# Gate and up projections of a feed-forward network: nine of eleven block pairs as seven products of quarters

## The chip, the cores and the metric

The kernel runs on one core of a Trainium2 chip. The metric is device time in microseconds (us) from one launch: 2508.59 us is the median of three runs of the kernel before (2506.43 to 2508.60). The profile is of one further execution.

## The reference

Two layers of a decoder trunk work on x of 512 tokens by 1024 features, all in float32. Each layer applies, with an RMS norm before and after each part, a feed-forward network (FFN), a hybrid token mixer (sparse attention and retention), cross-attention into 256 memory tokens, and a second FFN. What is changed here is the FFN:

```
def swiglu(x, w_gate, w_up, w_down):            # 1024 -> 2816 -> 1024
    return (jax.nn.silu(x @ w_gate) * (x @ w_up)) @ w_down
y = swiglu(rms_norm(x, pre_g), w_gate, w_up, w_down)
x = x + 0.5 * rms_norm(y, post_g)
```

There are four FFNs in all (two in each of two layers).

## The kernel before, in words

x lies in eight tiles of 128 features by 512 tokens (`x[c]`, features on the partitions), so a matmul has 128 x 128 weights as its stationary and up to 512 tokens as its moving operand. To keep float32 accuracy on a rounded type each operand is split into a high and a low part, and each product is three matmuls into one PSUM accumulation: high x high, high x low, low x high (`mm3`, L113 to L116).

Weights come as raw tiles of 128 x 1024 float32 (512 KB). `unit` (L79 to L87) loads one through SyncE's DMA queue into one of three `raw` buffers, ScalarE makes the high part `whi` (L85), and VectorE the low part `wlo` by a subtraction (L86); there are four buffers of each. GpSimd has no part in it.

`ffn` (L257 to L304) goes over the 22 blocks of 128 hidden features in three groups of 8, 7 and 7 (`GROUPS`). For a block it loads a gate unit and an up unit (8 slices of 128 x 128 each) and does 24 matmuls for each of the two, 48 of 512 columns. VectorE then multiplies both sums by the row norm `bc` (L274, L278), ScalarE takes a tanh (L276), VectorE finishes the SwiGLU (L279, L280), and the result is split into `hh` and `hl` (L122, L123). After a group the down projection adds the group's blocks to the eight tiles `y[c]`: units of 128 x 1024 or 128 x 896, one for each c, with 24 or 21 matmuls. In the last group each finished `y[c]` is squared on ScalarE and added up, mostly by GpSimd (`sumsq`, L145 to L155); `postnorm` (L205 to L213) makes the norm from it, updates x (VectorE `yn`, GpSimd `x`) and splits x for the next stage (`split_x`, L178 to L184). In the last FFN of the kernel `down_halves` does the last group for each half of the tokens apart, so that the first half's norm and output lie beside the second half's matmuls; its first block is also done in two halves of the tokens.

A stage before an FFN can leave it a `filler`: projections of memory keys or values that PE can do while the norm is made.

The order on each engine isn't the order of the text. A scheduler takes, at build time and with durations that it assumes, the instruction that comes first in the program among those that are ready and have a buffer; each engine then runs its list strictly in order. So work runs ahead as far as buffers reach: three `raw`, four `whi` and `wlo`, eight PSUM banks, and 24, 16 and 16 tiles of 128 x 512 in the classes "b", "xs" and "h".

Of the kernel before, what the change touches and what calls it, by code (L numbers as in the profile page):

```python
# [9 lines left out]
F32 = mybir.dt.float32  # L10
# [15 lines left out]
GROUPS = ((0, 8), (8, 15), (15, 22))  # L26
# [21 lines left out]
def trunk(ctx: ExitStack, tc: tile.TileContext, a: dict, out: bass.AP):  # L48
# [9 lines left out]
    slots = {"b": 24, "xs": 16, "h": 16, "kv": 6}  # L58
# [54 lines left out]
    def mm3(ps, ah, al, bh, bl, start, stop):  # L113
        pe.matmul(ps, ah, bh, start=start, stop=False)  # L114
        pe.matmul(ps, ah, bl, start=False, stop=False)  # L115
        pe.matmul(ps, al, bh, start=False, stop=stop)  # L116
# [40 lines left out]
    def rms_cols(ssq, n, width):  # L157
# [27 lines left out]

    def gcols(l, col):
        return small[l][:, col : col + NC]

    def prenorm():

        xh, xl = [h for h, _ in xs], [lo for _, lo in xs]
        xs.clear()
        ssq, part = None, None
# [9 lines left out]
        return xh, xl, cols, bc  # L203

    def postnorm(y, ssq, gains, nxt, ts_=slice(0, T)):  # L205

        w = ts_.stop - ts_.start
        ps = row_bc(rms_cols(ssq[:, ts_], D, w), w // P)
        for c in range(NC):
# [3 lines left out]
            split_x(c, nxt, ts_)  # L213
# [43 lines left out]
    def ffn(l, which, gains, nxt, filler=None, prep=None, halves=False):  # L257
        gu, dn = FF_UNITS[which]
        if filler:
            filler()  # L260
        xh, xl, cols, bc = prenorm()
        y, ssq = [None] * NC, None
        for gi, (f0, f1) in enumerate(GROUPS):
            hh, hl = [], []
            for f in range(f0, f1):
                w = [first.pop(b) if b in first else unit(a[gu][l, f, b], 1024) for b in range(2)]
                pss = [acc("ps_gu") for _ in range(2)]
# [18 lines left out]
            if prep and last:  # L286
                prep()
# [555 lines left out]
    for c in range(NC):  # L843
        split_x(c, gcols(0, G_F1PRE))
# [98 lines left out]
```

## Time and profile before

| | |
|---|---|
| median of three runs | 2508.59 us |
| the profiled execution | 2508.29 us, span 2506.5 us |
| PE busy | 2431.5 us (97%), 12052 matmuls |
| VectorE, ScalarE, GpSimd busy | 1400.2 (56%), 902.4 (36%), 258.8 us (10%) |
| DMA | 233.62 MB, mean 93 GB/s |
| TensorE clock granted | 0.995 in the mean |

All times in views are microseconds from the span's start. PE is TensorE's matmuls, PEld its weight loads, DVE is VectorE, ACT ScalarE, POOL GpSimd, SP SyncE. Matmuls overlap in the records, so their pace is read from the distance between starts. The FFNs take most of the span: their bodies lie at about 9 to 372, 900 to 1250, 1285 to 1635 and 2150 to 2490 us.

### The profile page before, as it was taken

The page shows a single profiled execution, that of the slowest core. Times are in us where ns is not written, and L with a number is a line of the kernel's source. Part 1 is how long each engine was busy: PE and PEld are TensorE (multiplying, and loading weights), DVE is VectorE, ACT ScalarE, POOL GpSimd, SP SyncE. Part 2 cuts the span into 40 slices and gives each one's busy share as a digit, 9 for nine tenths or more (in the row PEclk, how much of TensorE's full clock was granted, in tenths as well). Part 3 has the DMA queues.
Part 4 walks back from the last instruction along what each step waited for, and adds up shares of the span by engine and source line. Part 5 has one row for each costly group of instructions (what it writes and reads, how often), then busy time and mean ns, then how long its engine had stood idle before and what let it go on. Part 6 is the DMA issues. An engine that isn't in the chain of part 4 may idle for free. (4 is left out here: it accounts for less than half of the span.)

```text
span 2506.5 us, 30782 instructions
## 1 busy us (share of the span) xinstructions
PE 2431.5 (97%) x12052; PEld 2020.5 (81%) x12052; DVE 1400.2 (56%) x2536; ACT 902.4 (36%) x1480; POOL 258.8 (10%) x218
## 2 busy tenths in 40 slices
PE   8999999999999999999999999999999998999997
PEld 6888878888877878888878888868888777888887
DVE  6434458465776484344484344584657766634454
ACT  4322243255344443222343222332553443322222
POOL 0000022001040120000120000130010402100002
PEclk9999999999999999999999999999999999999999
DMA  4333333411232233233333333324112222232321
GB/s 173 98 100 94 99 121 108 143 45 34 76 109 84 93 101 93 101 93 100 110 98 96 101 93 101 106 89 150 44 35 70 93 76 68 86 100 92 102 90 62
DMA packets 74593, 233.62 MB, mean 93 GB/s; under 512 B 8272, under 2 KB 17744, under 8 KB 74448
## 3 DMA queue, kind: packets, MB, share of 16 engines
q1 hardware_dynamic: 65232, 222.21, 27.9%
q10 hardware_dynamic: 9216, 9.44, 1.2%
q8 instruction: 95, 1.56, 0.3%
q14 instruction: 50, 0.41, 0.1%
HBM read 229.53 MB, written 2.10 MB: 92 GB/s over the span
## 5 line engine op out<-in xcount | busy, mean ns | idle before, releaser
L85 ACT ACTIVATE whi<-raw 128x1024 fp32r<-128x1024 f32 (+2 forms) x402 | 417.8, 1041 | 1097.6 <-PE ps_gu L115 324.0
L86 DVE TENSOR_TENSOR wlo<-raw,whi 128x1024 fp32r<-128x1024 f32 (+2 forms) x402 | 491.2, 1223 | 292.7 <-ACT whi L85 284.4
L114 PE MATMUL ps_gu<-xsh,whi 128*128 128x512 f32 (+1 forms) x1424 | 552.3, 389 | 13.8 <-ACT whi L85 9.3
L115 PE MATMUL ps_gu<-xsl,whi 128*128 128x512 f32 (+1 forms) x1424 | 555.0, 390 | 9.9 <-DVE xsl L184 9.7
L116 PE MATMUL ps_gu<-xsh,wlo 128*128 128x512 f32 (+1 forms) x1424 | 552.8, 388 | 0.0
L115 PEld LDWEIGHTS ps_gu<-xsl,whi 128*128 128x128 f32 x1424 | 268.6, 189 | 71.2 <-DVE xsl L184 17.7
L114 PEld LDWEIGHTS ps_gu<-xsh,whi 128*128 128x128 f32 x1424 | 269.0, 189 | 69.2 <-ACT whi L85 9.2
L116 PEld LDWEIGHTS ps_gu<-xsh,wlo 128*128 128x128 f32 x1424 | 268.8, 189 | 55.4 <-DVE wlo L86 1.8
L154 POOL TENSOR_TENSOR ssq<-ssq,sq 128x512 f32<-128x512 f32 (+1 forms) x84 | 131.4, 1564 | 1708.7 <-ACT sq L153 1705.6
L115 PE MATMUL ps_dn<-hl,whi 128*128 128x512 f32 (+1 forms) x704 | 268.5, 382 | 2.4 <-DVE hl L123 2.4
L114 PE MATMUL ps_dn<-hh,whi 128*128 128x512 f32 (+1 forms) x704 | 268.2, 381 | 0.0
L116 PE MATMUL ps_dn<-hh,wlo 128*128 128x512 f32 (+1 forms) x704 | 268.0, 381 | 0.0
L278 DVE TENSOR_TENSOR u<-ps_gu,rstd_bc 128x512 f32<-128x512 f32 x88 | 60.8, 691 | 215.4 <-PE ps_gu L116 215.3
L274 DVE TENSOR_TENSOR g<-ps_gu,rstd_bc 128x512 f32<-128x512 f32 x88 | 60.8, 691 | 183.9 <-PE ps_gu L116 179.4
L115 PEld LDWEIGHTS ps_dn<-hl,whi 128*128 128x128 f32 x704 | 132.3, 188 | 28.9 <-DVE hl L123 3.8
L114 PEld LDWEIGHTS ps_dn<-hh,whi 128*128 128x128 f32 x704 | 132.4, 188 | 26.2 <-ACT hh L122 0.5
L116 PEld LDWEIGHTS ps_dn<-hh,wlo 128*128 128x128 f32 x704 | 132.4, 188 | 25.1
L301 DVE TENSOR_TENSOR y<-ps_dn,y 128x512 f32<-128x512 f32 x56 | 38.7, 691 | 132.3 <-PE ps_dn L116 132.3
L115 PE MATMUL ps_fm<-xsl,whi 128*128 128x512 f32 x256 | 103.2, 404 | 4.0 <-DVE xsl L184 3.8
L114 PE MATMUL ps_fm<-xsh,whi 128*128 128x512 f32 x256 | 103.0, 404 | 0.0
L116 PE MATMUL ps_fm<-xsh,wlo 128*128 128x512 f32 x256 | 101.3, 396 | 0.6 <-DVE wlo L86 0.6
L612 ACT ACTIVATE p<-p,smx 128x512 f32<-128x512 f32 (+3 forms) x128 | 70.5, 552 | 87.2 <-DVE smx L610 87.0
(226 smaller groups left out, 3723.0 us busy)
## 6 DMA issues: line engine op xcount, KB each, us to landing
raw<-in_ffn_gu_dram SPq DMA_DIRECT2D x176, 512.0 KB, 3.3
raw<-in_ffn_dn_dram SPq DMA_DIRECT2D x64, 448.0 KB, 3.3
raw<-in_ffn_dn_dram SPq DMA_DIRECT2D x32, 512.0 KB, 3.5
raw<-in_win_fm_dram SPq DMA_DIRECT2D x32, 512.0 KB, 3.3
raw<-in_wk_dram SPq DMA_DIRECT2D x16, 512.0 KB, 3.5
raw<-in_cmp_w_dram SPq DMA_DIRECT2D x16, 512.0 KB, 3.7
raw<-in_wout_dram SPq DMA_DIRECT2D x16, 512.0 KB, 3.5
raw<-in_wv_dram SPq DMA_DIRECT2D x16, 512.0 KB, 3.5
```

The source lines that it names most:

```text
L85: act.activation(hi, raw, AF.Copy)
L86: dve.tensor_tensor(lo, raw, hi.bitcast(F32), op=ALU.subtract)
L114: pe.matmul(ps, ah, bh, start=start, stop=False)
L115: pe.matmul(ps, ah, bl, start=False, stop=False)
L116: pe.matmul(ps, al, bh, start=False, stop=stop)
L154: eng.tensor_tensor(acc_t, acc_t, sq, op=ALU.add)
L274: dve.tensor_tensor(g1, pss[0], bc, op=ALU.mult)
L278: dve.tensor_tensor(u1, pss[1], bc, op=ALU.mult)
L301: dve.tensor_tensor(y[c], ps, y[c], op=ALU.add)
L612: act.activation(pr[i], pr[i], AF.Exp, bias=m, scale=-1.0, accum_out=sums[:, i : i + 1])
```

## The change

A pair of blocks is a 2 x 2 matrix of quarters: its rows are the two blocks, its columns the two halves of the 1024 inputs, and a quarter holds gate and up weights of 4 slices each, 128 x 1024 in all. x is a 2 x 2 matrix as well: halves of the inputs by halves of the tokens. Winograd's form of Strassen's scheme multiplies two such matrices with seven products of quarters instead of eight, and with sums of quarters before and after.

- `Pair` does this for nine of the eleven pairs of each FFN. Each product is 24 matmuls of 256 columns into one PSUM bank (gate in one half of it, up in the other). The sums of weights are made in place in the raw tiles by GpSimd: c + d into a new tile u, then c += a, u += a, u += b. Each of the seven raw tiles is then split as before. Partial results are kept by a copy on ScalarE (`kept`) or accumulate in PSUM, and VectorE and GpSimd combine them.
- The first two pairs of each FFN are plain: 48 matmuls of 256 columns for the first half of the inputs and 24 of 512 for the second, per block. While they run, `combos` makes the sums of x that the seven products need.
- The SwiGLU multiplies only the gate by the norm of the row; the factor that the up part lacks is put into the norm after the FFN (`cols` in `rms_cols`).
- The down projection comes in groups of four blocks and a last one of two. A group is done after the products of the following pair, and that pair's SwiGLU comes behind it. A unit of down weights now holds two c (or four).
- Buffers: six `raw` instead of three; "b" 18, "xs" 24, "h" 8. To fit, the mixer keeps q and ksel in raw tiles, and some of its and the attention's tiles move to "xs".
- The filler and the first two weight splits of the next FFN are now called at the start of the `postnorm` before it (`nxt[0]`).
- `down_halves` has two blocks instead of seven. The layout of the gate and up weights in DRAM follows the quarters.

```diff
-    slots = {"b": 24, "xs": 16, "h": 16, "kv": 6}
+    slots = {"b": 18, "xs": 24, "h": 8, "kv": 6, "onsa": 1}
...
-    def unit(src, n):
-        raw = wp.tile([P, 1024], F32, name="raw", tag="raw", bufs=3)[:, :n]
+    def raw_unit(src, n):
+        raw = wp.tile([P, 1024], F32, name="raw", tag="raw", bufs=6)[:, :n]
         nc.sync.dma_start(raw, src)
+        return raw
+    def split_unit(raw, n=1024):
         hi = wp.tile([P, 1024], F32R, name="whi", tag="whi", bufs=4)[:, :n]
         lo = wp.tile([P, 1024], F32R, name="wlo", tag="wlo", bufs=4)[:, :n]
         act.activation(hi, raw, AF.Copy)
         dve.tensor_tensor(lo, raw, hi.bitcast(F32), op=ALU.subtract)
         return hi, lo
-    def raw_unit(src, n):
-        raw = wp.tile([P, 1024], F32, name="raw", tag="raw", bufs=3)[:, :n]
-        nc.sync.dma_start(raw, src)
-        return raw
+    def unit(src, n):
+        return split_unit(raw_unit(src, n), n)
...
+    def split_s(c, g, ts_=slice(0, T)):
+        k = c % 4
+        for u, half in enumerate(HALVES):
+            if half.start < ts_.start or half.stop > ts_.stop:
+                continue
+            if c < 4:
+                if k % 2 == 0:
+                    ops["t", u] = big("x1h", F32R, tag="xs"), big("x1l", F32R, tag="xs")
+                ops[u + 1, k] = hi, lo = [t[:, HALVES[k % 2]] for t in ops["t", u]]
+                act.activation(hi, x[c][:, half], AF.Copy, scale=g[:, c : c + 1])
+                dve.scalar_tensor_tensor(lo, x[c][:, half], g[:, c : c + 1], hi.bitcast(F32), op0=ALU.mult, op1=ALU.subtract)
+        if c >= 4:
+            if ts_.start == 0:
+                ops["x", k] = big("x3h", F32R, tag="xs"), big("x3l", F32R, tag="xs")
+            hi, lo = [t[:, ts_] for t in ops["x", k]]
+            act.activation(hi, x[c][:, ts_], AF.Copy, scale=g[:, c : c + 1])
+            dve.scalar_tensor_tensor(lo, x[c][:, ts_], g[:, c : c + 1], hi.bitcast(F32), op0=ALU.mult, op1=ALU.subtract)
+            ops[3, k], ops[4, k] = [tuple(t[:, u] for t in ops["x", k]) for u in HALVES]
+    def combos(g):
+        sums = []
+        h7 = big("x7h", F32R, shape=(P, 4, T), tag="onsa")
...
+        for k in range(4):
+            b = []
+            for c in (k, k + 4):
+                xg = big("xg")
+                act.activation(xg, x[c], AF.Copy, scale=g[:, c : c + 1])
+                b += [xg[:, HALVES[0]], xg[:, HALVES[1]]]
+            t5, t7 = big("xt"), big("xt")
+            dve.tensor_tensor(t5[:, :256], b[1], b[0], op=ALU.subtract)
+            pool.tensor_tensor(t7[:, :256], b[3], b[1], op=ALU.subtract)
+            dve.tensor_tensor(t5[:, 256:], b[3], t5[:, :256], op=ALU.subtract)
+            pool.tensor_tensor(t7[:, 256:], t5[:, 256:], b[2], op=ALU.subtract)
+            put(5, k, t5, big("x5h", F32R, tag="xs"), big("x5l", F32R, tag="xs"))
+            sums.append(t7)
+        for k in range(4):
+            put(7, k, sums[k], h7[:, k], big("x7l", F32R, tag="xs"))
...
+    def postnorm(y, ssq, gains, nxt, ts_=slice(0, T), cols=None):
...
+        if ts_.start == 0 and nxt[0]:
+            nxt[0]()
...
+        def add(self, t, u):
+            pool.tensor_tensor(t, t, u, op=ALU.add)
+            return t
+        def raw(self, n):
+            if n == 1:
+                self.a = self.load(0)
+                return self.a
+            if n == 5:
+                self.c, self.d = self.load(2), self.load(3)
+                self.u = wp.tile([P, 1024], F32, name="raw", tag="raw", bufs=6)
+                pool.tensor_tensor(self.u, self.c, self.d, op=ALU.add)
+                return self.u
+            if n == 2:
+                self.b = self.load(1)
+                return self.b
+            if n == 7:
+                return self.add(self.c, self.a)
+            if n == 6:
+                return self.add(self.u, self.a)
+            if n == 3:
+                return self.add(self.u, self.b)
+            return self.d
+        def product(self, n, ps, o, start=True):
+            if n not in self.w:
+                self.weights(n)
+            wh, wl = self.w.pop(n)
+            for u in range(2):
+                for k in range(4):
+                    s = slice(u * 512 + k * P, u * 512 + (k + 1) * P)
+                    xh, xl = ops[o, k]
+                    mm3(ps[:, HALVES[u]], wh[:, s], wl[:, s], xh, xl, start and u == 0 and k == 0, u == 1 and k == 3, not start)
+        def kept(self, ps):
+            t = big("gk")
+            act.activation(t, ps, AF.Copy)
+            return t
...
+            for q in range(2):
+                k0 = "q", 2 * f + q
+                wh, wl = self.w.pop(k0) if k0 in self.w else split_unit(self.load(2 * f + q))
+                for k in range(4):
+                    for u in range(2):
+                        s = slice(u * 512 + k * P, u * 512 + (k + 1) * P)
+                        if q == 0:
+                            for i, half in enumerate(HALVES):
+                                mm3(pss[u][:, half], wh[:, s], wl[:, s], *ops[i + 1, k], i == k == 0, False)
+                        else:
+                            mm3(pss[u], wh[:, s], wl[:, s], *ops["x", k], False, k == 3)
...
+        def p1(self):
+            self.A = acc("ps_gu")
+            self.product(1, self.A, 1)
+            self.s1 = self.kept(self.A)
+        def p2(self):
+            self.product(2, self.A, 3, start=False)
+        def p7(self):
+            self.C = aux("ps_gc")
+            self.product(7, self.C, 7)
+            self.s7 = self.kept(self.C)
+        def p5(self):
+            self.B = acc("ps_gu")
+            self.product(5, self.B, 5)
+            self.s5 = self.kept(self.B)
+        def p6(self):
+            self.product(6, self.B, 6, start=False)
+            self.e = big("ge")
+            dve.tensor_tensor(self.e, self.B, self.s1, op=ALU.subtract)
+            pool.tensor_tensor(self.s5, self.e, self.s5, op=ALU.subtract)
+        def p4(self):
+            self.product(4, self.C, 8, start=False)
+            dve.tensor_tensor(self.s7, self.e, self.s7, op=ALU.subtract)
+            dve.tensor_tensor(self.s5, self.s5, self.C, op=ALU.subtract)
+        def p3(self):
+            ps = acc("ps_gu")
+            self.product(3, ps, 4)
+            dve.tensor_tensor(self.e, ps, self.e, op=ALU.subtract)
+        def swiglu(self, bc, hs, tag="h"):
+            for q in ((self.A, self.e), (self.s5, self.s7)):
+                g1, th = big("g1"), big("th")
+                for ts_, t in zip(HALVES, q):
+                    dve.tensor_tensor(g1[:, ts_], t[:, :256], bc[:, ts_], op=ALU.mult)
                 act.activation(th, g1, AF.Tanh, scale=0.5)
                 dve.scalar_tensor_tensor(g1, th, 1.0, g1, op0=ALU.add, op1=ALU.mult)
+                for ts_, t in zip(HALVES, q):
+                    dve.tensor_tensor(g1[:, ts_], g1[:, ts_], t[:, 256:], op=ALU.mult)
+                hs.append(split(g1, "h", 0.5, tag=tag))
...
+        ORDER = "p1", "p5", "p2", "p7", "p6", "p4", "p3"
...
+        def weights(f0, n):
+            per = 1024 // (n * P)
+            for c0 in range(0, NC, per):
+                raw = wp.tile([P, 1024], F32, name="raw", tag="raw", bufs=6)
+                nc.sync.dma_start(raw.rearrange("p (c n) -> p c n", c=per),
+                                  a[dn][l, c0 : c0 + per, :, f0 * P : (f0 + n) * P].rearrange("c p n -> p c n"))
+                wh, wl = split_unit(raw)
+                for u in range(per):
+                    yield c0 + u, [(wh[:, s], wl[:, s]) for s in
+                                   (slice((u * n + k) * P, (u * n + k + 1) * P) for k in range(n))]
...
+        hs = []
+        for p in pairs[:2]:
+            for f in range(2):
+                p.plain(f, bc, hs)
+                if p is pairs[0] and f == 1:
+                    combos(gcols(l, G_F1PRE if which == "ffn1" else G_F2PRE))
+        f0 = 0
+        for p in pairs[2:]:
+            final = p is pairs[-1]
+            for n in ORDER:
+                getattr(p, n)()
+            mine = []
+            if len(hs) == 4:
+                down(f0, hs, False)
+                f0, hs = f0 + 4, []
+            p.swiglu(bc, hs, "xs" if final else "h")
+        if prep:
+            prep()
+        if nxt is None:
+            down_halves(list(weights(f0, len(hs))), hs, y, gains, (cols, sq))
+            return
+        down(f0, hs, True)
+        postnorm(y, state["ssq"], gains, nxt, cols=(cols, sq))
...
+    xattn(0, (ffn_first(0, "ffn2", keys(1, 0, 4)), gcols(0, G_F2PRE)), filler=lambda: (mem_keys(0, 7, 8), mem_values(0, 0)), mid=values(0, 1), prep=split_mem(1))
+    ffn(0, "ffn2", half2[0], (ffn_first(1, "ffn1", keys(1, 4, 8)), gcols(1, G_F1PRE)), prep=split_mem(1))
...
+        o[w + "_gu"] = np.stack([np.stack([_tiles(f[f"{w}_w_gate"][l]), _tiles(f[f"{w}_w_up"][l])])
+                                 .reshape(2, NPAIR, 2, P, 2, 512).transpose(1, 2, 4, 3, 0, 5).reshape(NPAIR, 4, P, 1024)
                                  for l in range(DEPTH)])
```

## Rows read from the trace of the kernel before

**Rows 1.** The page: the span, and busy time of each engine.

```profile
span 2506.5 us, 30782 instructions
...
PE 2431.5 (97%) x12052; PEld 2020.5 (81%) x12052; DVE 1400.2 (56%) x2536; ACT 902.4 (36%) x1480; POOL 258.8 (10%) x218
```

**Rows 2.** Windows: us, busy (instructions) by engine, clock, DMA share, GB/s.

```profile
925.00:1215.00 290.00, 290.00 (x1281) 240.06 (x1281) 132.96 (x161) 83.41 (x104) 0.00 (x0) 1.00 0.30 96
1280.00:1290.00 10.00, 7.88 (x35) 5.69 (x34) 10.00 (x10) 2.30 (x3) 4.46 (x3) 1.00 0.17 57
2130.00:2140.00 10.00, 10.00 (x57) 9.54 (x57) 6.77 (x13) 7.34 (x15) 7.10 (x8) 0.74 0.01 2
```

**Rows 3.** PE's waits over the span: total us, times, longest.

```profile
PE ps_gu L115 <- DVE xsl L184: 9.7, 12, 1.4
...
PE ps_dn L115 <- DVE hl L123: 2.4, 3, 1.1
```

**Rows 4.** Timeline of PE at 512 columns: start, duration.

```profile
1299.71 0.39 PE L116 MATMUL ps_gu<-xsh,wlo 128*128 128x512 f32 x1
...
1305.83 0.39 PE L116 MATMUL ps_gu<-xsh,wlo 128*128 128x512 f32 x1
```

**Rows 5.** Timeline of PE at 256 columns.

```profile
2454.73 0.28 PE L116 MATMUL ps_dn<-hh,wlo 128*128 128x256 f32 x1
...
2466.25 0.28 PE L116 MATMUL ps_dn<-hh,dl 128*128 128x256 f32 x1
```

**Rows 6.** Timeline of DVE, beside POOL until 1284.61 and then alone.

```profile
1277.79 0.41 DVE L379 TENSOR_TENSOR mk<-ps_mk,mem_bc 128x256 f32<-128x256 f32 x1
1278.12 1.44 DVE L184 SCALAR_TENSOR_TENSOR xsl<-x,small,xsh 128x512 fp32r<-128x512 f32 x1
...
1279.82 1.98 DVE L86 TENSOR_TENSOR wlo<-raw,whi 128x1024 fp32r<-128x1024 f32 x1
1281.72 1.76 DVE L184 SCALAR_TENSOR_TENSOR xsl<-x,small,xsh 128x512 fp32r<-128x512 f32 x1
1283.40 1.77 DVE L154 TENSOR_TENSOR ssq<-ssq,sq 128x512 f32<-128x512 f32 x1
1285.09 0.74 DVE L184 SCALAR_TENSOR_TENSOR xsl<-x,small,xsh 128x512 fp32r<-128x512 f32 x1
1285.75 0.68 DVE L154 TENSOR_TENSOR ssq<-ssq,sq 128x512 f32<-128x512 f32 x1
...
1287.02 0.68 DVE L154 TENSOR_TENSOR ssq<-ssq,sq 128x512 f32<-128x512 f32 x1
1287.62 1.21 DVE L86 TENSOR_TENSOR wlo<-raw,whi 128x1024 fp32r<-128x1024 f32 x1
1288.76 0.68 DVE L198 TENSOR_TENSOR ssq<-ssq 128x512 f32<-128x512 f32 x1
```

**Rows 7.** Groups by line and shape, ACT: busy us, mean ns.

```profile
L85 ACT ACTIVATE whi<-raw 128x1024 fp32r<-128x1024 f32 x336 | 355.6, 1060 | 909.5 <-issue 301.8 <-PE ps_gu L115 235.1 <-PE ps_dn L115 168.8
```

**Rows 8.** Timeline of POOL in three places: adds beside DVE, then alone.

```profile
351.09 1.47 POOL L154 TENSOR_TENSOR ssq<-ssq,sq 128x512 f32<-128x512 f32 x1 [5.36 <-ACT sq L153]
354.74 1.29 POOL L154 TENSOR_TENSOR ssq<-ssq,sq 128x512 f32<-128x512 f32 x1 [2.18 <-ACT sq L153]
...
1278.97 5.64 POOL L154 TENSOR_TENSOR ssq<-ssq,sq 128x512 f32<-128x512 f32 x3
...
2485.95 0.74 POOL L154 TENSOR_TENSOR ssq<-ssq,sq 128x256 f32<-128x256 f32 x1 [1.38 <-ACT sq L153]
```

**Rows 9.** DMA issues: engine, count, KB each, us to landing.

```profile
raw<-in_ffn_gu_dram SPq DMA_DIRECT2D x176, 512.0 KB, 3.3
```

**Rows 10.** Timeline of PE at the entry of the last FFN.

```profile
2123.34 0.28 PE L116 MATMUL ps_gu<-xsh,wlo 128*128 128x256 f32 x1
...
2129.65 1.65 PE L114 MATMUL ps_gu<-xsh,whi 128*128 128x256 f32 x4 [2.82 <-ACT xsh L183]
```

**Rows 11.** Timeline of PE: the last down matmul.

```profile
2492.11 0.28 PE L116 MATMUL ps_dn<-hh,dl 128*128 128x256 f32 x1
```

More of the change, by code (lines that the diff above doesn't have):

```diff
@@ L111, in trunk, with mm3 @@
             lst.append(hg)
[L113 to L116, printed above, removed]
+    def mm3(ps, ah, al, bh, bl, start, stop, more=False):
+        pe.matmul(ps, ah, bh, start=start, stop=False, skip_group_check=more)
+        pe.matmul(ps, ah, bl, start=False, stop=False, skip_group_check=more)
+        pe.matmul(ps, al, bh, start=False, stop=stop, skip_group_check=more)
     def split(src, name, gain=None, tag="b"):
@@ L155, in sumsq, with rms_cols @@
         return acc_t
-    def rms_cols(ssq, n, width):
+    def rms_cols(ssq, n, width, cols=None):
         nt = width // P
@@ L192, in prenorm, with prenorm_rows @@
         xs.clear()
+        return xh, xl, *prenorm_rows()
+    def prenorm_rows():
         ssq, part = None, None
@@ L202, in prenorm @@
         act.activation(bc, ps, AF.Copy)
-        return xh, xl, cols, bc
-    def postnorm(y, ssq, gains, nxt, ts_=slice(0, T)):
+        return cols, bc
+    def postnorm(y, ssq, gains, nxt, ts_=slice(0, T), cols=None):
         w = ts_.stop - ts_.start
-        ps = row_bc(rms_cols(ssq[:, ts_], D, w), w // P)
+        if ts_.start == 0 and nxt[0]:
+            nxt[0]()
+        ps = row_bc(rms_cols(ssq[:, ts_], D, w, cols), w // P)
         for c in range(NC):
@@ L212, in postnorm @@
             (dve if c == 0 else pool).tensor_tensor(x[c][:, ts_], x[c][:, ts_], t, op=ALU.add)
-            split_x(c, nxt, ts_)
+            (split_s if nxt[0] else split_x)(c, nxt[1], ts_)
     def out_proj(src, l, oh, ol):
@@ L286, in ffn, with ffn_first, run @@
-            if prep and last:
-                prep()
-            if last and nxt is None:
-                down_halves(a[dn][l], f0, n, hh, hl, y, gains)
-                return
-            for c in range(NC):
-                wh, wl = unit(a[dn][l, c][:, f0 * P : f1 * P], n * P)
+                for ts_, t in zip(HALVES, q):
+                    dve.tensor_tensor(g1[:, ts_], g1[:, ts_], t[:, 256:], op=ALU.mult)
+                hs.append(split(g1, "h", 0.5, tag=tag))
+    warm = {}
+    def ffn_first(l, which, filler=None):
+        def run():
+            if filler:
+                filler()
+            ps_ = warm[l, which] = [Pair(a[FF_UNITS[which][0]][l], j) for j in range(NPAIR)]
+            for q in range(2):
+                ps_[0].w["q", q] = split_unit(ps_[0].load(q))
+        return run
@@ new lines, in ffn, with down @@
+    def ffn(l, which, gains, nxt, prep=None):
+        dn = FF_UNITS[which][1]
+        pairs = warm.pop((l, which))
+        y, state = [None] * NC, {"ssq": None}
+        ORDER = "p1", "p5", "p2", "p7", "p6", "p4", "p3"
[9 more added lines that the diff above has]
+                                   (slice((u * n + k) * P, (u * n + k + 1) * P) for k in range(n))]
+        def down(f0, hs, final):
+            n = len(hs)
+            for c, w in weights(f0, n):
@@ L687, in to_fm @@
                 pe.transpose(pt[:, i * P : (i + 1) * P], tiles[i], ident)
-            h_, l_ = split(pt, "o", sm[:, G_NSA + c : G_NSA + c + 1], tag="h")
+            h_, l_ = split(pt, "o", sm[:, G_NSA + c : G_NSA + c + 1], tag="xs" if c < 4 else "h")
             oh.append(h_)
@@ L818, in xattn @@
                     mm3(ps, v_h[:, fs], v_l[:, fs], pTh[m], pTl[m], m == 0, m == 1)
-                h_, l_ = split(ps, "xo", tag="h")
+                h_, l_ = split(ps, "xo", tag="xs" if f < 4 else "h")
                 oh.append(h_)
```

138 lines of the change are left out of this document (63 added, 75 removed).

## The prediction

> **What bounds the kernel now.** I read the page's busy shares first. TensorE (PE) is busy 2431.5 of 2506.5 us, and 75.0 us are left for every other cause [rows 1]. A busy PE can still be a stalling one, so the second view is the windows over the body of one feed-forward network (FFN): 290.00 of 290.00 us of PE at clock 1.00, VectorE (DVE) 132.96 (46%), ScalarE (ACT) 83.41 (29%), GpSimd (POOL) nothing [rows 2]. The third is the list of waits. PE's stalls in an FFN are some microseconds, and they sit at its entry (the splits of x, 9.7 us in 12 waits) and before its last down group (2.4 us in 3) [rows 3]. So the FFN bodies go at the pace of matmul issue, and only two things can change their time: fewer or shorter matmuls, or another engine that falls behind PE. That engine has to be looked for on DVE and POOL.
>
> **The matmuls.** The pace is the distance between starts, since the durations overlap. At 512 columns, 27 steps take 1305.83 - 1299.71 = 6.12 us, 0.2267 us each [rows 4]. At 256 columns, 96 steps take 2466.25 - 2454.73 = 11.52 us, 0.1200 us each [rows 5]. Half the columns cost 53% of the time, so seven products for eight don't give an eighth.
> - A pair of blocks (two of gate, two of up) was 96 matmuls of 512: 21.76 us. As seven products it is 7 x 24 of 256: 20.16 us. Saved: 1.60 us, for 36 pairs (9 in each of 4 FFNs) 57.6 us.
> - The 16 blocks that stay plain do the first half of K in halves of the tokens: 48 of 256 (5.76) and 24 of 512 (5.44), 11.20 us where 48 of 512 were 10.88. Cost: 16 x 0.32 = 5.1 us.
> - In the last FFN the first block was already done as 96 of 256 (11.52 us, which the 11.20 above replaces: another 0.6 us less than counted).
> - The last down group was 336 of 256 (7 blocks, 40.32 us). Now five of these blocks run at 512 columns (120, 27.20 us) and two in halves (96, 11.52 us): 1.6 us less. All other down matmuls stay as they were.
>
> Sum on PE: -57.6 + 5.1 - 0.6 - 1.6 = **-54.7 us**. That comes only if nothing else becomes late.
>
> **DVE and POOL in a pair.** What a DVE instruction takes out of the queue is the step to the next start: 1.14 us at 1024 columns, 0.60 at 512, 0.33 at 256 [rows 6]. A pair of seven products needs on DVE: 7 wlo (7.98), four 512-wide subtractions (2.40), eight 256-wide products of the SwiGLU (2.64), and twice an add-multiply and a low part (2.40): 15.4 us beside 20.16 us of PE. Its share of the down projection, half of a group of four blocks, is 48 matmuls of 512 (10.88 us of PE) with 2 wlo and 4 sums into y: 4.7 us. Bare, DVE has 20.1 us of work in 31.0, 65% against 46% before: hidden. ACT has 9 whi of 1.06 us [rows 7] and seven smaller ones; even at 1.06 each, 17 us of 31: hidden.
>
> POOL was idle here and gets four sums of 128x1024 and one of 128x512 per pair. No row shows that width. A 256-wide add takes 0.74 us and a 512-wide one 1.29 to 1.47 [rows 8]; the same slope gives 2.4 to 2.9 us, and I take 2.6, which makes 4 x 2.6 + 1.3 = 11.7 us per pair. In a pair's 20.16 us of products POOL is no bound of itself. The longest chain runs through u: landing 3.3 us [rows 9], then three times sum, whi and wlo (2.6 + 1.06 + 1.14), 17.7 us bare; with six raw buffers the next pair's chain starts while this one ends.
>
> What decides is that POOL and DVE slow each other. While POOL does three 512-wide adds in 5.64 us (1.88 each instead of 1.29 to 1.47) [rows 8], the DVE instructions with two SBUF inputs step 1.90, 1.68 and 1.69 us instead of 1.14, 0.66 and 0.60 [rows 6]: 2.87 us late in three adds, 0.96 per 512 columns of POOL. The mk product, with an input in PSUM, keeps its 0.33 beside POOL. Of a pair's 20.1 us of DVE some 5 have a PSUM input, and some POOL work meets an idle DVE, so I take half to all of it: 0.5 to 0.96 per 512 columns, nine of these per pair, 4.5 to 8.6 us. DVE then has 24.6 to 28.7 us of work in 31.0: on average it still fits. Where it doesn't is the stretch of two pairs between two down groups: DVE 2 x 15.4 + 9.0 to 17.2 = 39.8 to 48.0 us against 40.32 of PE, a backlog of 0 to 7.7. It meets a reserve: with four whi/wlo buffers a product's weights can be split three products ahead, 3 x 2.88 - 1.06 - 1.14 = 6.4 us. What exceeds it stalls PE: 0 to 1.3 us per stretch, and the down group behind it (21.8 us of PE, 9.4 of DVE) gives the reserve back. There are 16 such stretches, four in each FFN. Ahead of them a single pair follows the plain blocks, whose second pair (22.4 us of PE) has 9.4 us of DVE of its own, 7.4 for the sums of x (8 of 256, 8 of 512) and up to 3.8 for their eight narrow POOL adds, 20.6 in all: just hidden. The order on DVE is fixed at build time, and an early place behind a late POOL sum holds up all that follows. I take 1.0 us per stretch and 0.5 for each single pair, **+18 us**, with 0 and 54 (3.4 per stretch, the whole gain) as ends, since no row shows this mix.
>
> In the Trainium skill, "SBUF — State Buffer", section "SBUF: two separate sides", the port pair shared by DVE and POOL is an exclusive lock, held for the whole instruction, against DVE instructions with two SBUF inputs. The 0.8 to 1.1 us by which each of the three is late, beside adds that take 1.3 us alone, agree with a lock better than with shared bandwidth. By that rule a wider add would hold DVE longer at a time; that is the second rival below.
>
> **What moves.**
> - Entries. The first block now takes x slice by slice: 12 matmuls of 0.12 us (1.44 us) per slice in its first half of K where it took three of 0.2267 (0.68). DVE gives a slice each 1.7 us under POOL [rows 6], so a slice's wait falls from about 1.0 to 0.3 us: over the 12 waits of [rows 3] 4 us less over start and two entries (0 to 8). The last FFN's entry had its own order, all of the first token half before the second; it ran until 2123.34, waited until 2129.65 and then ran in part at the lower of PE's two clock levels, 1.2 of 2.4 GHz (mean 0.74 in 2130 to 2140) [rows 2, 10]. Now both halves alternate slice by slice, so early matmuls can queue behind the later half: 0 to 7 us, taken as 2. The fillers (memory keys) only move from after the postnorm to before it; they are ready in both places.
> - Ends of the other FFNs. The wait for hl before the last down group (2.4 us) goes, since that group now follows a whole group of 21.8 us. In return the last group has 1.36 us of PE per row of y beside a POOL add of 1.3 to 1.9, so the norm's sum comes up to 3 us later. Zero together, -2 to +4.
> - The end. From the last down matmul to the end are 2506.5 - 2492.1 = 14.4 us [rows 1, 11]. The second half had 20.2 us of matmuls over the first half's norm and output; now it has 5.8, so about 4.5 us of DVE work for the first half's output meets the second half's chain: +2 (0 to 5).
> - Mixer and attention swap buffer classes (q, ksel, vr, gr, o) with counts that come out equal: 0, up to +5 if the 18 remaining "b" buffers or three raw ones bind.
> - Down weights come in pieces of 2 KB instead of 4 and are 512 KB per 5.4 us of PE, loaded ahead: 0.
>
> Sum: the profiled execution took 2508.29 us (span 2506.5 and 1.8 around it; the median of the three runs is 2508.59). 2508.3 - 54.7 + 18 - 4 + 2 + 2 = **2471.6 us**, forecast 2471.
>
> **Rivals.**
> 1. PE never waits in the pairs: the reserve covers all. 2471.6 - 18 = 2453.6. For it: the backlog ends at 0 by the lower rate, and DVE's mean is 65% bare. Against it: where DVE is full beside POOL (10.00 of 10 us, 1280 to 1290), PE does 7.88 of 10 [rows 2]. Chance 0.27 (2446 to 2459).
> 2. DVE, held by POOL, becomes the bound of the pairs: slower. Place: the second pair of each stretch. If a 1024-wide sum holds a DVE instruction for its whole 2.6 us, a pair loses 11.7 us, the backlog is 30.8 + 23.4 - 40.3 = 13.9 and the stall 7.5 us per stretch, 120 us in 16: about 2574. It decides against the change from 3.4 us per stretch, a backlog of 9.8, a loss of 9.7 us per pair or 1.07 per 512 columns; the narrow adds gave 0.96 [rows 6, 8]. So near the edge: for it the width, against it the PSUM inputs and idle times that hide a part. Chance 0.13 of over 2513.
> 3. The pairs stall about 3.4 us per stretch and eat the gain: 2453.6 + 54 = 2507.6. Chance 0.05 of 2503 to 2513.
>
> The forecast's own band, 2459 to 2503 (0.2 to 2.7 us per stretch, small terms at their ends), has 0.55. Holding 8 in 10 takes in rival 1 and the upper edge: 2448 to 2515. A measurement of this kernel can't tell less than 0.2% (5 us) from no change. Faster by more, under 2503.5: 0.55 + 0.27 = 0.82; same 0.05; slower 0.13.
>
> **What will show it.** In an FFN body: matmuls of 256 columns in steps of 0.120 us, seven products in 20.2 us; if the step is longer with PE unhindered, the first term is wrong. DVE busy at 80 to 92% there. PE waits on wlo or whi of 0 to 3 us per stretch, in the second pair more than in the first. POOL sums of 2.6 us alone and up to 3.8 beside DVE; wlo at 2 to 3 us during one. The prediction is wrong if PE's waits for weights add up to more than 54 us, if the clock falls inside the bodies, or if PE waits for POOL sums or raw loads rather than for DVE.

## The result: 2593.0 us, 3.4% slower

The changed kernel takes 2593.02 us (median of 4 runs, 2588.28 to 2596.85) where the kernel before takes 2507.51 (2505.92 to 2508.60): a ratio of 1.0341, interval 1.0318 to 1.0363. Its runs lie 8.6 us apart, so what a single edit gains below is known to some 6 us. The forecast was 2471, with 2515 as the upper end. The page of the profiled run, span and engines, against [rows 1]:

```profile
span 2594.7 us, 37728 instructions
...
PE 2420.1 (93%) x14860; PEld 2145.4 (83%) x14860; DVE 1915.5 (74%) x3018; ACT 1105.2 (43%) x1760; POOL 740.6 (29%) x430
```

PE was idle for 75.0 us before and is for 174.6 now. PE's waits (total us, times, longest), against [rows 3]:

```profile
PE ps_gu L121 <- ACT gk L379: 45.8, 20, 4.1
PE bc_ps L185 <- DVE rs_y L148: 24.9, 11, 4.5
...
PE rms_ps L169 <- DVE ssq L161: 12.0, 3, 10.4
...
PE ps_fm L123 <- DVE wlo L89: 4.6, 3, 2.9
```

The largest wait is for `gk`, the copy that `kept` makes of product 1 on ACT, and not for weights. To see where all 88.3 us of the two spans' difference (2594.74 against 2506.46) are, I cut both timelines of PE at the first matmul of each group of gate and up products, at each down group, and at the next FFN's first matmul, and took from each piece its matmuls by pitch (0.2267 and 0.1200 us, [rows 4, 5]). What is left over:

| piece | before | after | difference | predicted |
|---|---|---|---|---|
| matmuls by pitch | | | -54.7 | -54.7 |
| 16 stretches of two pairs, 40.32 us of matmuls each | | 63.4 | +63.4 | +16 |
| first group of each FFN (plain blocks, first pair) | 34.3 | 57.1 | +22.8 | 0 (-4 + 2 + 2) |
| from an FFN's last down group, its matmuls off, to the next FFN's first matmul | 1008.1 | 1054.1 | +46.0 (22.3, 7.6, 16.1) | 0 |
| last down group to the end, its matmuls off | 15.4 | 25.9 | +10.5 | +2 |
| start | 9.25 | 9.51 | +0.3 | 0 |

The differences add up to the 88.3 us. The first row agrees by construction, since it is the counts of both traces times the forecast's pitch; what bears the pitch out are pieces without a stall: the down groups between stretches last 21.79 us where 96 x 0.2267 is 21.76, and the stretches of e1 and e10 below 40.31 where 336 x 0.1200 is 40.32. Every term of what stands between the matmuls was too small.

**The stretches.** Windows of the changed kernel (us, busy and instructions of PE, PEld, DVE, ACT, POOL, clock, DMA share, GB/s), against the bodies in [rows 2]: four stretches and the down groups between them; the first, the second and the last of these stretches alone; and ten microseconds behind the first one's stall.

```profile
1013.81:1255.94 242.13, 230.78 (x1633) 218.45 (x1632) 207.62 (x218) 101.94 (x125) 92.75 (x37) 0.99 0.32 99
1013.81:1060.54 46.73, 42.38 (x338) 41.96 (x337) 43.08 (x44) 22.29 (x29) 18.27 (x8) 0.96 0.35 102
1082.32:1126.57 44.25, 41.91 (x337) 41.70 (x336) 36.70 (x35) 19.95 (x24) 18.95 (x8) 0.96 0.36 108
1213.04:1255.94 42.90, 40.57 (x337) 40.36 (x336) 36.62 (x35) 19.84 (x24) 17.31 (x7) 1.00 0.38 115
1044.50:1054.50 10.00, 9.94 (x70) 9.95 (x71) 8.02 (x8) 4.67 (x7) 3.24 (x1) 0.83 0.50 139
```

The last stretch, with 40.32 us of matmuls, lasts 42.90, and DVE is busy for only 36.62 of them: here it is no bound, and so in 12 of the 16. The first stretch of each FFN is another case: DVE is busy for 43.1 of 46.7 us, more than PE has to do. There PE waits 4.1 us for the copy, in the other twelve stretches 2.33 to 2.35, and a lower clock follows behind all four of the longer waits (0.83 in the last row) and behind four of the shorter (0.96 in the third). The 16 waits are 44.4 of the 63.4 us, and most of the rest lies in the eight stretches in which the clock fell. This is one of the waits of 2.33, in the timelines (start, duration) of POOL, DVE, ACT and PE:

```profile
1229.39 1.29 POOL L425 TENSOR_TENSOR gk<-ge,gk 128x512 f32<-128x512 f32 x1 [1.83 <-DVE ge L424]
1232.44 2.41 POOL L340 TENSOR_TENSOR raw<-raw 128x1024 f32<-128x1024 f32 x1 [1.76 <-DVE wlo L89]
...
1229.50 1.72 DVE L429 TENSOR_TENSOR gk<-ge,gk 128x512 f32<-128x512 f32 x1
1231.15 1.21 DVE L89 TENSOR_TENSOR wlo<-raw,whi 128x1024 fp32r<-128x1024 f32 x1
...
1232.88 3.05 DVE L89 TENSOR_TENSOR wlo<-raw,whi 128x1024 fp32r<-128x1024 f32 x1
1235.85 0.68 DVE L435 TENSOR_TENSOR ge<-ps_gu,ge 128x512 f32<-128x512 f32 x1
...
1239.31 0.42 DVE L446 TENSOR_TENSOR g<-g,ge 128x256 f32<-128x256 f32 x1
...
1237.02 0.63 ACT L443 ACTIVATE th<-g 128x512 f32<-128x512 f32 x1 [2.64 <-DVE g L442]
1237.56 1.04 ACT L88 ACTIVATE whi<-raw 128x1024 fp32r<-128x1024 f32 x1
1239.76 0.63 ACT L132 ACTIVATE hh<-g 128x512 fp32r<-128x512 f32 x1 [1.16 <-DVE g L446]
1240.30 0.61 ACT L443 ACTIVATE th<-g 128x512 f32<-128x512 f32 x1
1240.82 0.58 ACT L379 ACTIVATE gk<-ps_gu 128x512 f32<-128x512 f32 x1
...
1241.45 0.39 PE L121 MATMUL ps_gu<-x3h,whi 128*128 128x256 f32 x1 [2.33 <-ACT gk L379]
```

Read it upwards. Product 2 adds onto product 1's bank, so it waits for the copy at 1240.82. The copy needs nothing but ACT, and stands in ACT's list behind `th` and `hh` of the SwiGLU of the pair before. These waited 2.64 and 1.16 us for DVE, which had lost 1.04 us in the subtraction at 1229.50 (1.72 us beside POOL's 1.29, where such a one takes 0.68 alone [rows 6]) and 1.84 in the low part at 1232.88 (3.05, where the one before takes 1.21). A wide sum on POOL takes 2.35 to 2.41 us at its shortest and 2.8 on the average; 2.6 alone was worked out from [rows 8].

### The profile page after: what moved, and what is told of

Read it like the earlier page. It is cut to its first block, busy times and chain, and to the rows that moved or that the text cites. A ratio compares the mean times of both kernels' runs of the same rounds, so it can differ in the third digit from the quotient of the medians.

```text
span 2594.7 us, 37728 instructions
## 1 busy us (share of the span) xinstructions
PE 2420.1 (93%) x14860; PEld 2145.4 (83%) x14860; DVE 1915.5 (74%) x3018; ACT 1105.2 (43%) x1760; POOL 740.6 (29%) x430
## 4 chain that ended last, share of the span: by engine, by line
PE 72%; DVE 18%; ACT 3%; issue 3%; POOL 1%; DMA 1%; ACTq 0%; DVEq 0%; SPq 0%; POOLq 0%
PE ps_gu L121 6%; PE ps_gu L122 6%; PE ps_gu L123 6%; DVE wlo L89 6%; PE ps_dn L121 6%; PE ps_dn L122 6%; PE ps_dn L123 6%; PE ps_po L833 3%; PE ps_o L121 2%; PE ps_o L122 2%; PE ps_o L123 2%; PE ps_gc L122 2%; PE ps_gc L121 2%; PE ps_gc L123 2%; PE ps_fm L123 2%
## 5 line engine op out<-in xcount | busy, mean ns | idle before, releaser
L89 DVE TENSOR_TENSOR wlo<-raw,whi 128x1024 fp32r<-128x1024 f32 (+1 forms) x506 | 750.8, 1485 | 285.4 <-ACT whi L88 284.0
L88 ACT ACTIVATE whi<-raw 128x1024 fp32r<-128x1024 f32 (+1 forms) x506 | 532.2, 1054 | 672.3 <-PE ps_gu L122 155.0
L340 POOL TENSOR_TENSOR raw<-raw 128x1024 f32<-128x1024 f32 x108 | 304.8, 2822 | 516.2 <-DVE wlo L89 492.4
L121 PE MATMUL ps_gu<-x3h,whi 128*128 128x256 f32 (+1 forms) x704 | 222.9, 317 | 45.8 <-ACT gk L379 45.8
L122 PE MATMUL ps_gu<-x3l,whi 128*128 128x256 f32 (+1 forms) x704 | 221.1, 314 | 0.3
L123 PE MATMUL ps_gu<-x3h,wlo 128*128 128x256 f32 (+1 forms) x704 | 220.3, 313 | 0.0
L121 PEld LDWEIGHTS ps_gu<-x3h,whi 128*128 128x128 f32 x704 | 141.5, 201 | 54.7 <-ACT gk L379 49.8
L121 PE MATMUL ps_gc<-x7h,whi 128*128 128x256 f32 x576 | 163.7, 284 | 1.0 <-ACT gk L379 1.0
L123 PE MATMUL ps_gc<-x7h,wlo 128*128 128x256 f32 x576 | 163.4, 284 | 0.0
L122 PE MATMUL ps_gc<-x7l,whi 128*128 128x256 f32 x576 | 163.1, 283 | 0.0
L122 PE MATMUL ps_gu<-x5l,whi 128*128 128x256 f32 x576 | 163.0, 283 | 0.0
```

Of the source, the lines that this page charges most:

```text
L88: act.activation(hi, raw, AF.Copy)
L89: dve.tensor_tensor(lo, raw, hi.bitcast(F32), op=ALU.subtract)
L121: pe.matmul(ps, ah, bh, start=start, stop=False, skip_group_check=more)
L122: pe.matmul(ps, ah, bl, start=False, stop=False, skip_group_check=more)
L123: pe.matmul(ps, al, bh, start=False, stop=stop, skip_group_check=more)
L340: pool.tensor_tensor(t, t, u, op=ALU.add)
```

## The experiments

Each is an edit of the changed kernel, shortened here; its time is set against 2593.0. The kernel before took 2508.1 to 2509.4 us beside them.

**e1: the SwiGLU behind the next pair's product 2.**

```
 for n in ORDER:
     getattr(p, n)()
+    if n == "p2" and late: late.swiglu(bc, hs); late = None
 if len(hs) == 4: ... p.swiglu(...)
+else: late = p
```

> The only edit: where no down group lies between two pairs, the SwiGLU of the first is issued after the second pair's product 2 instead of ahead of its product 1. In the changed kernel the stretches of two pairs take 40.3 us of matmuls by pitch and last 42.9 to 47.9, 63 us too long over 16 stretches, 45.8 us of it one wait per stretch of product 2 for the kept copy of product 1. Theory A (ScalarE's list is in order: the kept copy stands behind tanh and high part of the SwiGLU before it, and these wait for a late VectorE): the waits on kept copies fall from 45.8 to under 10 us, the stretches to 40.3 to 41.5, the time by 35 to 60 us, to 2535 to 2558. Theory B (VectorE has more work in a stretch than PE has, so the wait can only move): PE waits as long for low parts or subtractions instead, the time stays within 15 us of 2593.

2539.1 us, 53.9 less. What is left of the waits for kept copies, and one stretch:

```profile
PE ps_gc L121 <- ACT gk L379: 4.5, 8, 0.9
PE ps_gu L121 <- ACT gk L379: 1.4, 4, 0.8
```

```profile
1188.12:1228.43 40.31, 40.31 (x337) 40.31 (x336) 35.02 (x34) 19.95 (x24) 16.86 (x7) 1.00 0.39 118
```

All sums are still there, DVE is as busy (1911.7 us in all), and the stretch has lost nothing: theory A, and theory B falls. The first stretch of each FFN keeps 1.7 us and the down group behind it 0.8, with DVE busy for 40.8 of the stretch's 42.0 us; there DVE's load is not ruled out as the cause.

**e2: no weight sums.**

```
-pool.tensor_tensor(t, t, u, op=ALU.add)      # add: returns t as it is
-self.u = wp.tile([P, 1024], F32, name="raw", ...)
-pool.tensor_tensor(self.u, self.c, self.d, op=ALU.add)
+self.u = self.d
```

> Leaves out all five weight sums of a pair on GpSimd and takes an unsummed quarter in place of each (so five of seven products have other weights); all loads, splits, products and subtractions stay. Theories A and B both: without the sums VectorE's low parts of weights go back from 1.49 to about 1.2 us, the waits for kept copies fall from 45.8 to under 10 us and the time by 35 to 60 us, to 2535 to 2558. Rival C (the wait is the chain product 1, copy, product 2 itself and has nothing to do with a late VectorE): the waits stay at 40 or more and the time within 10 us of 2593.

2511.1 us, 81.9 less, more than either theory said. The sums are four per pair, not five, and without them four of the seven products have other weights; the tile u and the chain of loads and sums through it are gone too. Stretches last 40.47 us, so rival C falls. That it is POOL's work beside DVE, and not u or the chain, is for e8, which keeps both. Of the 28 us beyond e1, 20 are in the first groups of the FFNs, at their entries: 71.4 us where two took 77.6 and 77.7, 83.9 for 90.6, 69.9 for 71.0.

**e3: the fillers behind the norm's transposes.**

```
-if ts_.start == 0 and nxt[0]: nxt[0]()
 ps = row_bc(rms_cols(ssq[:, ts_], D, w, cols), w // P)
+if ts_.start == 0 and nxt[0]: nxt[0]()
```

> The only edit: the fillers (memory keys, first splits of the next FFN) are issued behind the norm's two sets of transposes instead of ahead of them. Theory: issued ahead, the fillers run first and leave PE nothing beside the norm's chain; from the last matmul before the norm to the first matmul of the next FFN it took 13.1 and 13.2 us in the kernel before and takes 21.8 and 22.2 in the changed one. With the edit both are back at 13 to 15 us: 14 to 18 us less in all, 2575 to 2580. Rival (the chain through VectorE is what lasts 22 us, since it also splits x into narrower pieces): each shrinks by less than 3 us, time within 6 us of 2593.

2581.8 us, 11.2 less, short of the theory's 14 to 18. In the changed kernel PE does the filler first and then has nothing beside the norm's chain:

```profile
1288.38 0.39 PE L123 MATMUL ps_dn<-hh,wlo 128*128 128x512 f32 x1
1288.61 0.28 PE L121 MATMUL ps_mk<-memg,whi 128*128 128x256 f32 x1
...
1300.12 0.60 PE L169 MATMUL rms_ps<-cst,ssq 128*128 128x128 f32 x4
1305.29 1.11 PE L185 MATMUL bc_ps<-cst,rs_y 128*128 128x128 f32 x4 [4.57 <-DVE rs_y L178]
1310.56 1.22 PE L121 MATMUL ps_gu<-x1h,whi 128*128 128x256 f32 x4 [4.16 <-ACT x1h L211]
```

With the edit this piece (last down group to first matmul) falls from 54.6 to 48.3 us, the other one by 9.9, and the two entries behind them give back 1.7 and 2.6.

**e4: a last group of four blocks.**

```
-down(f0, hs, False)
-f0, hs = f0 + 4, []
+n = 2 if final and nxt is None else 4
+down(f0, hs[:n], False)
+f0, hs = f0 + n, hs[n:]
```

> The only edit: in the last FFN the down group before the last takes two blocks and the last one, which is done in token halves, takes four instead of two. 0.6 us more of matmuls. Theory: with two blocks a half has 5.8 us of matmuls over the norm and output of the first half, and the chain through ScalarE's squares, GpSimd's sums and VectorE ends 25 us after the last down matmul instead of 14.4; with four blocks (11.5 us per half) that is 16 to 19 us, and the time falls by 5 to 9 us, to 2584 to 2588. Rival (VectorE and GpSimd have the same work in either case and set the end): within 3 us of 2593.

2583.5 us, 9.5 less, a little more than the theory's 5 to 9; behind the last group's matmuls there are 18.6 us instead of 25.9, so 7.3 of the 9.5 are seen at the end itself. In the changed kernel, with two blocks, PE ends its second half long before the sum of squares is there, and 25.2 us pass from its last down matmul to the end, where it was 14.4 [rows 11]:

```profile
2569.55 0.28 PE L123 MATMUL ps_dn<-hh,wlo 128*128 128x256 f32 x1
2570.81 0.43 PE L185 MATMUL bc_ps<-cst,rs_y 128*128 128x128 f32 x2 [0.98 <-DVE rs_y L178]
2581.62 0.69 PE L169 MATMUL rms_ps<-cst,ssq 128*128 128x128 f32 x2 [10.38 <-DVE ssq L161]
```

**e5: q and ksel in tiles of class h.**

```
-q = pair_tile("q") + pair_tile("q")
+q = [big("q", tag="h") for _ in range(4)]      # ksel likewise, two
```

> The only edit: the mixer's q and ksel go from halves of three raw tiles to six tiles of class h, which stand free there, so six raw buffers instead of three serve its weights. Theory: the three held raw tiles make loads late; PE's stretch from the mixer's first projection matmul to its first matmul on values took 55.9 us (409.7 to 465.6 would be as before; it is 73.9) and 81.5 us, where the kernel before needed 66.5 and 68.0. With the edit both are back at 66 to 70 us: 10 to 20 us less in all, 2573 to 2583. Rival (the fillers and the norm ahead of it leave VectorE late, the buffers are enough): under 4 us less.

2584.6 us, 8.4 less, under the theory's 10 to 20. From the first projection matmul to the first on values the two mixers took 66.5 and 67.9 us in the kernel before, 73.9 and 81.4 in the changed one (the expectation's 55.9 is a slip) and now take 69.6 and 71.0, 14.7 us less, so the buffers are the cause there. A part comes back in the heads, where the wait for q grows from 2.1 to 5.8 us; why is not settled.

**e6: the first pair's sums on DVE.**

```
+self.eng = dve if j == 2 else pool            # in Pair; both sums use it
```

> The only edit: the weight sums of the first pair with seven products of each FFN run on VectorE instead of GpSimd (four of 128x1024). In the changed kernel two of GpSimd's sums (2.36 and 2.35 us) fall into the norm at an FFN's entry, and two 128x4 instructions of the Newton steps, 0.16 us otherwise, take 2.23 and 2.19 us beside them; PE waits 4.1 us for the result and then runs for some microseconds at the lower clock. Theory (a GpSimd sum holds any VectorE instruction with two SBUF inputs for its whole length): the held steps are gone, each of three entries gets 4 to 7 us shorter (77.6 to about 72), 10 to 20 us in all, 2573 to 2583. Rival (the entry is bound by the additions to x and the splits, VectorE's own sums of 1.14 us take the same time there): within 4 us of 2593.

2572.8 us, 20.2 less, at the theory's upper end; the entries last 72.2, 72.0 and 84.1 us. PE's waits for the norm's result were 24.9 us in 11 and are:

```profile
PE bc_ps L185 <- DVE rs_y L148: 12.6, 10, 4.3
```

What the entries lost before, in the timelines of DVE and POOL in the changed kernel:

```profile
1333.58 0.16 DVE L146 SCALAR_TENSOR_TENSOR rs_u<-rs_t,rms_v 128x4 f32<-128x4 f32 x1
1333.78 2.31 DVE L148 SCALAR_TENSOR_TENSOR rs_y<-rs_u,rs_y 128x4 f32<-128x4 f32 x1
1336.12 0.16 DVE L144 TENSOR_TENSOR rs_t<-rs_y 128x4 f32<-128x4 f32 x1
1336.32 2.19 DVE L146 SCALAR_TENSOR_TENSOR rs_u<-rs_t,rms_v 128x4 f32<-128x4 f32 x1
...
1333.71 2.35 POOL L351 TENSOR_TENSOR raw<-raw 128x1024 f32<-128x1024 f32 x1 [6.38 <-DVE rs_t L144]
1336.14 2.35 POOL L340 TENSOR_TENSOR raw<-raw 128x1024 f32<-128x1024 f32 x1
```

Four columns take as long as POOL's 1024, twice in a row, in the chain whose result PE waits for.

**e8: all sums on DVE**: `pool.tensor_tensor` becomes `dve.tensor_tensor` in `add` and in product 5's sum.

> All four 128x1024 weight sums of a pair run on VectorE, none on GpSimd; the order of ScalarE's list stays. In the traces of the changed kernel and of the one without sums VectorE is busy 1915 and 1709 us: being held costs 5.7 us per pair; the sums done by itself are 4 x 1.14 = 4.6 us. If what counts is VectorE's mean load, this is about the changed kernel: 2575 to 2595. If what counts is that a GpSimd sum holds the one instruction that ScalarE or the norm waits for, waits on kept copies fall by half or more and the entries get shorter: 2535 to 2570. If VectorE becomes the bound of the stretches (2 x 20 us of its own plus the down group's share, of 40.3): above 2600.

2520.9 us, 72.1 less, better than all three forecasts; three of four stretches last 41.17 us, with one wait of 0.6. Groups of DVE (count, busy us, mean ns):

```profile
L89 DVE TENSOR_TENSOR wlo<-raw,whi 128x1024 fp32r<-128x1024 f32 (+1 forms) x506 | 626.9, 1240 | 264.9 <-ACT whi L88 263.3
L340 DVE TENSOR_TENSOR raw<-raw 128x1024 f32<-128x1024 f32 x108 | 131.5, 1218 | 1.0
```

The same groups where POOL does the sums:

```profile
L89 DVE TENSOR_TENSOR wlo<-raw,whi 128x1024 fp32r<-128x1024 f32 (+1 forms) x506 | 750.8, 1485 | 285.4 <-ACT whi L88 284.0 <-PE bc_ps L185 0.5
L340 POOL TENSOR_TENSOR raw<-raw 128x1024 f32<-128x1024 f32 x108 | 304.8, 2822 | 516.2 <-DVE wlo L89 492.4 <-DMA raw<-in_ffn_gu_dram 21.0
```

DVE is busy for 1862.3 us in this run, for 1915.5 with the sums on POOL and for 1709.0 without sums (e2). By these differences being held by 144 sums costs DVE 206 us, doing them 153. Tile u and the chain of sums are all there, so the lateness came from POOL's work beside DVE.

**e9: each sum as four adds of 256 columns on POOL.**

```
-pool.tensor_tensor(t, t, u, op=ALU.add)
+for i in range(4):
+    s = slice(i * 256, (i + 1) * 256)
+    pool.tensor_tensor(t[:, s], t[:, s], u[:, s], op=ALU.add)
```

> The only edit: each 128x1024 weight sum of the changed kernel is issued on GpSimd as four adds of 128x256. Same amount of work, a quarter of the width. If the length of a single GpSimd instruction is what hurts (a held VectorE instruction waits at most for one add, 0.74 us alone), the held 128x4 steps at the entries fall from 2.2 to under 1 us, the waits on kept copies from 45.8 to under 25 us and the time by 20 us or more, to under 2573. If the amount of GpSimd work beside VectorE is what hurts (each of the four adds holds another instruction), more steps are held for less each, the waits stay at 35 us or more and the time at 2580 to 2615.

2580.0 us, 13.0 less; the kept copies' wait 39.7 us in 18. By both signs it is the second theory, the time at its very edge. The Newton steps in this run, with POOL's adds beside them:

```profile
1329.97 0.17 DVE L148 SCALAR_TENSOR_TENSOR rs_y<-rs_u,rs_y 128x4 f32<-128x4 f32 x1
1330.17 0.70 DVE L144 TENSOR_TENSOR rs_t<-rs_y 128x4 f32<-128x4 f32 x1
1330.90 0.66 DVE L146 SCALAR_TENSOR_TENSOR rs_u<-rs_t,rms_v 128x4 f32<-128x4 f32 x1
1331.60 0.65 DVE L148 SCALAR_TENSOR_TENSOR rs_y<-rs_u,rs_y 128x4 f32<-128x4 f32 x1
...
1330.11 2.79 POOL L355 TENSOR_TENSOR raw<-raw 128x256 f32<-128x256 f32 x4 [6.00 <-DMA raw<-in_ffn_gu_dram]
```

Seven steps in a row take 0.65 to 0.70 us now (three are shown), where two of 2.2 were held: each add holds one instruction for its own length, so narrow adds cure little. Nor is it the total: DVE is busy for 1834.0 us here, 81.5 less than with whole sums and less than in e8, which is 59 us faster (POOL is busy for 929.8 instead of 740.6). So the total of the held time does not set PE's waits; that it matters which instruction is held is likely, but no run tries it apart.

**e7: e1, e3, e4, e5 and e6 together**, and the last FFN's first block with all K on one token half first:

```
+for i, half in enumerate(HALVES):             # plain, first block
+    for u in range(2):
+        for q, (wh, wl) in enumerate(ws): ... mm3(pss[u][:, half], ..., *ops[2 * q + i + 1, k], ...)
```

> Six edits together: SwiGLU behind product 2, fillers behind the norm, last down group of four, mixer buffers of class h, first sums on VectorE, and the last FFN's first plain block done for all K on the first token half before the second, as in the kernel before (0.6 us more of matmuls). The first three alone gave 54, 11 and 9.5 us. If the gains add, with 10 to 20 us each for the next two and 0 to 8 for the last: 2593 - 54 - 11 - 9.5 - 15 - 15 - 4 = 2485, between 2470 and 2500: 0.3 to 1.5% faster than the kernel before. If they overlap (edits that take away the same lost time), 2500 to 2520: no faster.

2496.2 us, ratio to the kernel before 0.9950 (0.9936 to 0.9963). The five single gains add up to 103.2 us, and 96.8 were had with the sixth edit, which was not tried alone: entries behind a moved filler are again 75.6 and 77.7 us long. The last FFN's entry takes 82.1 us, 2.1 less than in e6.

**e10: e7 with all sums on DVE as in e8, and e11: the same without the edit of e1.**

> The six edits of the kernel that took 2496 us, but all weight sums on VectorE instead of the first pair's alone. There the stretches of two pairs and the down groups behind them still lose 2.5 us in the first stretch of each FFN and 0.2 in the others, 12 us in all; with VectorE's sums alone they lost 0.9 in three of four, 10 us. Theory (what is left there comes from held instructions and from ScalarE's order, one cured by each edit): both together lose under 4 us, 2484 to 2490. Rival (VectorE with 20 us of its own work in a pair of 20.2 us of matmuls becomes the bound): 2496 or more.

> The same as the kernel with six edits and all sums on VectorE, but with the SwiGLU of a pair ahead of the next pair's product 1, as in the changed kernel. Theory: with VectorE in time the order of ScalarE's list costs little, 0.9 us in three of four stretches as in the run with all sums on VectorE alone: 8 to 12 us more than with the later SwiGLU. Rival (with VectorE's own sums the order makes no difference, or an early SwiGLU is better since it is spread): within 4 us of it or less.

e10: 2488.5 us, ratio 0.9921 (0.9908 to 0.9935), as its theory said. e11: 2495.9 us, 0.9955 (0.9943 to 0.9968), 7.4 more than e10, a little under the 8 to 12 of the theory. In e10 all 16 stretches last 40.31 or 40.32 us; the window of one:

```profile
1171.36:1211.67 40.31, 40.31 (x337) 40.30 (x336) 34.48 (x40) 19.96 (x24) 2.80 (x2) 1.00 0.39 119
```

In e11 twelve of the 16 keep 0.84 to 0.90 us, as in e8. So what was left in e7's and e8's stretches comes from both, DVE's lateness and ACT's order.

**e12: e10 with the norms' additions on DVE.**

```
-(dve if c == 0 else pool).tensor_tensor(x[c][:, ts_], x[c][:, ts_], t, op=ALU.add)
+dve.tensor_tensor(x[c][:, ts_], x[c][:, ts_], t, op=ALU.add)
-ssq = sumsq(ssq, x[c], c, pool)               # prenorm_rows, c < 4
+ssq = sumsq(ssq, x[c], c, dve)
```

> The kernel of 2488.5 us, with one more move from GpSimd to VectorE: the seven additions to x of each postnorm and the three sums of squares of each prenorm (128x512; 1.3 to 1.5 us each on GpSimd, 0.66 on VectorE by the rows of both engines alone). At the entries VectorE's low parts of x take 1.74 and 1.76 us instead of 0.68 beside these additions, and PE waits 1.75 to 2.0 us for them. Theory (a VectorE instruction that is held by a GpSimd one loses more than doing the addition itself): the entries of the FFNs, 77.6, 76.5 and 81.7 us for 65.0 to 65.6 us of matmuls, get 2 to 5 us shorter and so do the entries of mixer and attention: 2465 to 2483. Rival (the work in series on VectorE is longer than on two engines): 2489 or more.

2484.6 us, 0.9903 (0.9886 to 0.9919), the lowest time; 3.9 under e10, less than the theory's 5.5 to 23.5, and the intervals overlap, so it is not shown to be faster than e10. PE's waits for low parts of x fell (`x3l` from 7.5 to 1.8 us, `xsl` of the attention from 4.7 to 2.5), but the FFNs' entries are not shorter (77.3, 76.7 and 84.8 us against 77.6, 76.5 and 81.7): the wait for the norm's Newton chain grew from 8.8 to 20.2 us. What was saved in one wait came back in another.

## Why the prediction was wrong

- **Matmuls, -54.7: right.** Pitch and counts hold; e10 shows stretches of 336 x 0.1200 us.
- **DVE's load: right in size.** The hold is 206 us over 144 sums, 1.43 us each or 0.72 per 512 columns; 0.5 to 0.96 was predicted. In 12 of the 16 stretches DVE was not the bound (36.6 of 42.9 us); in the first of each FFN its busy time, 43.1 us, did exceed PE's 40.3, and of these stretches e1 left 1.7 us each.
- **Stalls in the pairs, +18: the step that failed.** It set DVE's backlog against a reserve of weights split ahead and let only the excess reach PE, 1.0 us per stretch and 0.5 per single pair. The low parts were indeed early enough: PE hardly waits for `wlo` in the pairs. But a late DVE also makes tanh and the high part of the SwiGLU late, ACT works its list in order, and the copy that product 2 needs stands behind them. That path has no reserve. It cost 4.0 us per stretch, 63.4 in all; e1 got 53.9 back by order alone. "Even at 1.06 each, 17 us of 31: hidden" judged ACT by its mean load and did not ask what its list waits for.
- **Entries, -4 + 2: wrong sign.** They lost 22.8 (0.8, 4.9, 4.3 and 12.8 in the four FFNs). I priced only the splits of x and not the first sums of the first pair, which fall into the norm: e6 takes 18.5 us off the entries. What it leaves lies near the forecast: with the matmuls off the first three are 2.0 us shorter than in the kernel before (4 was forecast), the last is 6.3 longer (2, up to 7, for the new order of its halves).
- **Fillers, 0: wrong.** "They are ready in both places" is true, but ahead of the norm they use up what covered its chain: at least 11.2 us (e3).
- **The mixer's buffers, 0 to +5: too small**, 8.4 (e5). **The end, +2 (0 to 5): too small**, +10.5, of which e4 gives 7.3 back.
- **The rivals.** Rival 2 had the sign, the hold for a whole sum and the break-even of 3.4 us per stretch (4.0 came, so the pairs alone ate the gain, as in rival 3), but its way, DVE as the bound, is not what happened in 12 of 16 stretches (36.62 of 42.90 us); in the other four it may have had a share. The signs named for a wrong prediction were waits for weights over 54 us, a lower clock in the bodies and waits for POOL or loads; the clock sign showed, the decisive wait was on none of them. Of what lies between FFNs (+46.0), e3 and e5 account for about 20 us; in e7, with both, these pieces are still 16.6 us longer than before, and where that goes was not tried apart.

## What to carry to other kernels

Before work goes to an idle engine, look at what its instructions do to their neighbour: here a sum on POOL made DVE busy for longer (1.43 us, 206 over 144) than doing it itself did (1.06, 153 over 144). And follow each wait through the order of every engine on its way: a copy that needs nothing is as late as the latest thing ahead of it in its list, whatever the mean load. Work that is ready at either of two places still has a price where it is taken from, if it covered a chain there.

## What the runs showed of the hardware

In these traces a DVE instruction with two SBUF inputs that starts beside a POOL add is held until the add ends: 128x4 steps of 0.16 us took 2.19 to 2.31 us beside sums of 2.35, and 0.65 to 0.70 beside adds of 256 columns, one per add; a low part of 128x1024 ended 1.08 us behind the sum beside it and took 3.05 us instead of 1.21. This is what the Trainium skill, "SBUF — State Buffer", section "SBUF: two separate sides", calls an exclusive lock for the whole instruction; these rows agree, with DVE instructions of 4 columns and of 1024. PE's granted clock was 0.83 over the ten microseconds behind a wait of 4.1 us although PE was busy for 9.94 of them: it fell to the lower of its two levels (0.50 from 1046 to 1048 us, 1.2 of 2.4 GHz). Behind the twelve waits of 2.33 to 2.35 us it fell in four stretches, of 44.2 to 44.4 us, and stayed at 1.00 in the other eight, of 42.9; in e10, without these waits, it was 1.00 in all 16.
